# A transformer block with expert retrieval: one dense block's keys and gates brought forward in the last group, six shared PSUM banks

## The chip, the cores and the metric

The kernel runs on one core of a Trainium2 chip. The metric is the device time of one execution in microseconds. The engines are TensorE (PE; its weight loads are PEld), VectorE (DVE), ScalarE (ACT), GpSimd (POOL) and SyncE (SP), which here only issues transfers. Each engine works through its own instructions in order. All times of engines below are from one profiled execution.

## The reference

One block over 1024 tokens of width 1024. The first half mixes tokens (an mLSTM and a differential attention side by side); the second half, which matters here, is a retrieval of experts:

```python
y = jnp.concatenate([hm, od], axis=-1) @ w_out[l]
x = x + g1 * y
h2 = rmsnorm(x, norm2_g[l]) * (1.0 + sc2) + sh2
x = x + g2 * peer(h2, ...)

def block(xb):                      # 128 tokens
    q = (xb @ w_query).reshape(128, 8, 2, 128)
    s = jnp.einsum('thpk,hpnk->thpn', q, sub_keys)
    sv, si = lax.top_k(s, 16)
    cand = sums of all 16 x 16 pairs;  fv, fpos = lax.top_k(cand, 16)
    eidx = jnp.take_along_axis(cidx, fpos, axis=-1)
    g = jax.nn.softmax(fv, axis=-1)
    u = u_tab[eidx]
    act = gelu(jnp.einsum('td,thkd->thk', xb, u))
    return jnp.einsum('thk,thkd->td', g * act, v_tab[eidx])
```

Each token has 8 heads, each head picks 16 of 16384 experts (128 x 128 product keys), and each expert is one row of u and one of v. The result goes through a last rmsnorm.

## The kernel before

The 1024 tokens are 8 blocks tb of 128, worked in three groups of 2, 3 and 3 blocks (GROUPS). A group runs through the front: norm1 (its `dr` at line 357), projections (`ps_pj`, lines 391 and 411, weights `wr` loaded by SyncE), convolution and mLSTM, attention in units that each end with an operation `ae` (line 606) and its transposes `ps_at` (line 617), output projection, norm2 (again `dr`), and product keys: queries, scores `ps_s` (line 862), the tops of 16 per half (lines 891 to 895) and `route`, which yields each token's expert numbers and gates.

Experts are computed in two ways. The blocks tb 0, 1, 6 and 7 gather: GpSimd fetches rows of u and v (`gu`, `gv`, `gvr`), VectorE takes the products with u (line 1010), and the sums with v are done on TensorE (`ga`, line 1072) for tb 0 and 1 and on VectorE for 6 and 7 (line 1046). The blocks tb 2 to 5 (DENSE) are computed against all 16384 experts in the dense phase, which starts when the front has ended. For each of 128 rows j of 128 experts: `s_mm` loads u, splits it into two parts `us` (lines 1312 and 1313), runs 24 matmuls `ps_dS` (line 1320) and a Gelu; `s_gate` multiplies the result by the gates `Gt` and splits it into `W`; `v_step` loads and splits v (`dvs`) and runs the matmuls `ps_dA` (line 1352). Products run 14 rows ahead (AHEAD) of the gates.

The dense phase wants gates as a full matrix, tokens by experts, with zeros for what was not picked. `gates()` makes it from the picked numbers: for each block, after a transposition `ps_gt`, 32 steps of a one-hot `oh` on VectorE (two operations, lines 1237 and 1238, in two buffers), 8 small matmuls `ps_g` (line 1224) and an evacuation into the staging tile `stg` (line 1226), which has one buffer. After every four steps SyncE sends the staging tile, 1 MB, to `G_d` in memory (line 1229). In the front, `gates()` is a background: a generator that is advanced by so many steps at each tick, a tick being a load of weights in a projection. The number per tick is RP. `all_gates` takes the first three dense blocks, tb 2 to 4, in the front; the fourth, tb 5, is in the last group, and its gates are made inside the dense phase, between the first rows of `s_mm`. While that is so, the second part of `us` is made by GpSimd for the first 18 rows, and `Gt` is loaded in two parts.

The front's matmuls write into five PSUM banks (`psb`); a sixth bank (`psq`) belongs to the gates. The order of the instructions on each engine is set when the kernel is built, by a scheduler of the framework that plays the program through on a model of the engines, within the order of priority in which it is written.

Of the kernel before, what the change touches and what calls it, by code (L numbers as in the profile page):

```python
# [8 lines left out]
F32 = mybir.dt.float32  # L9
# [12 lines left out]
P = 128  # L22
# [29 lines left out]
def kernel(ctx: ExitStack, tc: tile.TileContext, x, c_col, ada_w, ada_b, ada_bc, n1c,  # L52
# [3 lines left out]
    WB, T2, C8, KV, T4, RB, SB, OB, WLO, PB, LAG, DB, GD, AHEAD, LG, RH, ORDL, UP, LP, L0, DU, HP, HJ = 7, 8, 4, 2, 3, 3, 1, 2, 0, 5, 4, 2, 1, 14, 3, 4, 1, 18, 310000, 3, 28, 0, 0  # L56
# [13 lines left out]
    RG, RP = 1.6, 1.5  # L70
# [9 lines left out]
    psq = front_ctx.enter_context(tc.tile_pool(name="psq", bufs=6 - PB, space=PSUM))  # L80
# [30 lines left out]
    def gbank(name):  # L111
        return psq.tile([P, 512], F32, tag="pg", name=name)
# [729 lines left out]
    def front_keys(o, found):  # L842

        n, nb = o.n, o.nb
        o.rt = [route_start() for _ in range(nb)]
        for g in range(4):
            if g == N1G and o.k + 1 < len(gs):
                front_norm1(gs[o.k + 1])
# [9 lines left out]
            proj_T(wq, g * 512, o.h2T, nb, q_evac)  # L858
            for b in o.order:
                ps = bank("ps_s")  # L860
                for f in range(4):
                    nc.tensor.matmul(ps[:, f * P:(f + 1) * P], q[f][:, b * P:(b + 1) * P], sk[:, f],
                                     start=True, stop=True)
                if b == o.put_off:
                    if g == 0:
                        kept = fr.tile([P, 16, P], F32, tag="stg", name="s", bufs=SB)
                    s = kept[:, g * 4:g * 4 + 4]
                else:
                    s = fr.tile([P, 4, P], F32, tag="t2", name="s", bufs=T2)
                nc.scalar.activation(s, ps.rearrange("p (f n) -> p f n", f=4), AF.Copy)  # L870
                if b != o.put_off:
                    key_tops(o, b, g, s, found)
        if o.put_off is not None:
            for g in range(4):
                key_tops(o, o.put_off, g, kept[:, g * 4:g * 4 + 4], found)
# [252 lines left out]
    def all_gates():  # L1128
        while gating or not ended:
            if gating and gating[0][2] < sum(tb < starts[-1] for tb in DENSE):  # L1130
                yield from gates(*gating.pop(0))
            elif ended:
                return
# [300 lines left out]
    for k, o in enumerate(gs):  # L1434
# [7 lines left out]
        def found(b, h0=0, nh=PH):  # L1442
            tb, r = o.t0 + b, o.rt[b]
            dense_ = tb in DENSE
            route(r, dense_, tb in MIXED or (dense_ and last), h0, nh)
# [14 lines left out]
        o.put_off = o.order[-1] if k == 0 and DEF else None  # L1460
# [81 lines left out]
```

## Time and profile before

| | us |
|---|---|
| median of 3 runs | 3025.44 (3018.88 to 3027.79) |
| the profiled execution | 3014.83 |
| its span in the trace | 3012.7 |

| engine | busy, us | share of the span |
|---|---|---|
| TensorE | 2795.3 | 93% |
| VectorE | 2382.6 | 79% |
| GpSimd | 1280.1 | 42% |
| ScalarE | 971.3 | 32% |

The profiled execution is one run, and 10.6 us shorter than the median of the others. The span is what the trace covers. A busy share is a mean over stages: the table of stretches further down cuts the last group's front and the dense phase apart. A float32 matmul of the front leaves two records in the trace, and so does a gu; a ps_g, a dS and a dA leave one.

### The profile page before, as it was taken

What the parts mean: (1) busy time and instruction counts of PE and PEld (TensorE: products, weight loads), DVE (VectorE), ACT (ScalarE), POOL (GpSimd) and SP (SyncE); (2) the same over time, 40 slices, a digit from 0 to 9 for tenths busy, and PEclk for the clock granted to TensorE, in tenths of its full rate; (3) what the DMA queues carried; (4) which work ended last, traced back from release to release, by engine and by line L of the source; (5) the groups of instructions that cost most, each with busy time, mean ns of one, the idle gap of its engine ahead of it and who ended that gap; (6) DMA issues with size and microseconds to landing.
All of it is one profiled execution on the core that took longest, in us unless ns stands there. A gap on an engine that the chain in (4) does not pass through costs nothing.

```text
span 3012.7 us, 40060 instructions
## 1 busy us (share of the span) xinstructions
PE 2795.3 (93%) x13686; PEld 2087.7 (69%) x13686; DVE 2382.6 (79%) x5489; ACT 971.3 (32%) x1692; POOL 1280.1 (42%) x1083
## 2 busy tenths in 40 slices
PE   6899999599999989999797999999999999999998
PEld 5547757375566756665475877788777787777886
DVE  5634999847997677356998988899888899888956
ACT  1432244311244444222443322323222223222332
POOL 0000366654565443334556555455444454444300
PEclk9989999699999979999798999999999999999999
DMA  8745699899999887988799999999999999999942
GB/s 281 248 141 178 227 359 331 312 365 337 321 347 323 298 296 275 342 318 312 281 312 321 332 323 320 336 343 322 330 321 335 326 344 321 322 317 311 307 140 70
DMA packets 396848, 900.00 MB, mean 299 GB/s; under 512 B 34770, under 2 KB 184274, under 8 KB 392548
## 3 DMA queue, kind: packets, MB, share of 16 engines
q0 software_dynamic: 147456, 536.94, 49.6%
q1 hardware_dynamic: 249188, 360.51, 35.8%
q8 instruction: 108, 1.77, 0.2%
q14 instruction: 96, 0.79, 0.1%
HBM read 846.97 MB, written 50.35 MB: 298 GB/s over the span
## 4 chain that ended last, share of the span: by engine, by line
PE 44%; DVE 27%; DMA 15%; issue 9%; ACT 2%; POOL 2%; SPq 0%; DVEq 0%; POOLq 0%; ACTq 0%
PE ps_pj L391 10%; PE ps_pj L411 8%; PE ps_dA L1352 7%; DVE gu L1010 7%; DMA Gt<-G_d 6%; PE ps_dS L1320 6%; DVE ga L1046 4%; PE ps_g L1224 3%; PE ga L1072 3%; DMA gu<-in_peer_u_dram,ei 2%; DVE dvs L1346 2%; PE ps_S L593 2%; DVE dacc L1359 2%; DVE us L1313 2%; DVE W L1331 1%
## 5 line engine op out<-in xcount | busy, mean ns | idle before, releaser
L1006 POOL DMA_INDIRECT gu<-in_peer_u_dram,ei x512 | 651.7, 1273 | 958.7 <-DVE sv L894 346.6
L1352 PE MATMUL ps_dA<-dvs,W 128*128 128x512 f32 x2976 | 718.5, 396 | 46.2 <-DVE dvs L1346 18.5
L1320 PE MATMUL ps_dS<-dhT,us 128*128 128x512 f32 x3072 | 733.4, 393 | 11.1 <-POOL us L1313 8.9
L1010 DVE SCALAR_TENSOR_TENSOR gu<-gu,h2r 128x1024 f32<-128x1024 f32 x512 | 630.0, 1241 | 74.6 <-DMA gu<-in_peer_u_dram,ei 66.0
L1352 PEld LDWEIGHTS ps_dA<-dvs,W 128*128 128x128 f32 x2976 | 566.2, 191 | 176.5 <-DVE dvs L1346 22.3
L1320 PEld LDWEIGHTS ps_dS<-dhT,us 128*128 128x128 f32 x3072 | 581.7, 190 | 138.2 <-POOL us L1313 10.3
L1039 POOL DMA_INDIRECT gvr<-in_peer_v_dram,ei x256 | 302.4, 1181 | 314.2 <-DVE ga L1046 178.3
L1058 POOL DMA_INDIRECT gv<-in_peer_v_dram,eT x256 | 274.6, 1073 | 263.1 <-PE ga L1072 143.1
L1046 DVE SCALAR_TENSOR_TENSOR ga<-gvr,w,ga 128x1024 f32<-128x1024 f32 x254 | 325.3, 1281 | 1.5 <-DVE us L1313 0.4
L1345 ACT ACTIVATE dvs<-dv 128x512 fp32r<-128x512 f32 x248 | 155.2, 626 | 323.3 <-PE ps_dA L1352 169.7
L391 PE MATMUL ps_pj<-hT,wr 128*128 128x384 f32 (+1 forms) x768 | 234.7, 461 | 2.8 <-ACT ae L586 2.6
L391 PE MATMUL ps_pj<-h2T,wr 128*128 128x384 f32 (+1 forms) x768 | 231.2, 454 | 0.0
L1321 ACT ACTIVATE ge<-ps_dS 128x512 f32<-128x512 f32 x128 | 76.5, 598 | 441.7 <-PE ps_dS L1320 430.2
L1226 ACT ACTIVATE stg<-ps_g 128x512 f32<-128x512 f32 x128 | 133.9, 1065 | 242.4 <-PE ps_g L1224 162.9
L391 PEld LDWEIGHTS ps_pj<-hT,wr 128*128 128x128 f32 x768 | 145.4, 194 | 79.9 <-issue 9.0
L1329 DVE SCALAR_TENSOR_TENSOR ge<-ge,Gt 128x512 f32<-128x512 f32 x128 | 86.5, 685 | 137.2 <-DMA Gt<-G_d 115.2
L391 PEld LDWEIGHTS ps_pj<-h2T,wr 128*128 128x128 f32 x768 | 142.2, 190 | 74.4 <-issue 11.1
L411 PE MATMUL ps_pj<-wr,hT 128*128 128x256 f32 (+1 forms) x672 | 179.9, 421 | 4.6 <-DMA wr<-in_w_in_dram 3.7
L1346 DVE TENSOR_TENSOR dvs<-dv,dvs 128x512 fp32r<-128x512 f32 x248 | 168.1, 682 | 16.9 <-ACT dvs L1345 16.9
L1237 DVE TENSOR_TENSOR oh<-iotah,dT 128x1024 f16<-128x1024 f16 x128 | 92.0, 724 | 111.7 <-PE ps_g L1224 90.4
L1224 PE MATMUL ps_g<-oh 128*128 128x128 f16 x1024 | 138.6, 296 | 33.3 <-DVE oh L1238 14.5
L1072 PE MATMUL ga<-gv,strip 128*32 128x256 f32 x2048 | 150.7, 410 | 15.4 <-DMA gv<-in_peer_v_dram,eT 11.7
(292 smaller groups left out, 3304.0 us busy)
## 6 DMA issues: line engine op xcount, KB each, us to landing
u<-in_peer_uT_dram SPq DMA_DIRECT2D x128, 512.0 KB
dv<-in_peer_v_dram SPq DMA_DIRECT2D x248, 256.0 KB
wr<-in_w_in_dram SPq DMA_DIRECT2D x168, 256.0 KB
G_d<-stg SPq DMA_DIRECT2D x32, 1024.0 KB
Gt<-G_d SPq DMA_DIRECT2D x15, 2048.0 KB
wmod<-in_ada_w_dram SPq DMA_DIRECT2D x48, 512.0 KB
wr<-in_peer_w_query_dram SPq DMA_DIRECT2D x96, 256.0 KB
wr<-in_w_out_dram SPq DMA_DIRECT2D x48, 256.0 KB
```

Of the source, the lines that this page charges most:

```text
L391: nc.tensor.matmul(out[f], w2[:, kh, f * P:(f + 1) * P], hT[:, kb, :n], start=kb == 0 and f % k == 0, stop=kb == NC - 1 and f % k == k - 1)
L411: nc.tensor.matmul(out[f], hT[:, kb, f * P:(f + 1) * P], wk[:, kh], start=kb == 0 and f % k == 0, stop=kb == NC - 1 and (f % k == k - 1 or ...
L1006: nc.gpsimd.indirect_dma_start(out=u, out_offset=None, in_=pu, in_offset=bass.IndirectOffsetOnAxis(ap=o.ei[:, k:k + 1], axis=0))
L1010: nc.vector.scalar_tensor_tensor(u, u, 1.0, o.h2, op0=OP.mult, op1=OP.mult, accum_out=o.z[:, k:k + 1])
L1039: nc.gpsimd.indirect_dma_start(out=vt, out_offset=None, in_=pv, in_offset=bass.IndirectOffsetOnAxis(ap=o.ei[:, k:k + 1], axis=0))
L1046: nc.vector.scalar_tensor_tensor(o.acc, vt, o.w[:, k:k + 1], o.acc, op0=OP.mult, op1=OP.add)
L1058: got = nc.gpsimd.indirect_dma_start(out=vt, out_offset=None, in_=pv, in_offset=bass.IndirectOffsetOnAxis(ap=o.eT[:, t:t + 1], axis=0))
L1072: mm = nc.tensor.matmul(o.acc[c * 32:(c + 1) * 32, q * QW:(q + 1) * QW], st[:, q, 31 + 32 * i - r:63 + 32 * i - r], vt[:, c * QW:(c + 1) * ...
L1224: nc.tensor.matmul(pg[:, r * P:(r + 1) * P], oh[:, 0, :, r], oh[:, 2 + i, :, r], start=i == 0, stop=i == np_ - 1)
L1320: nc.tensor.matmul(ps, us[:, a, c], hT[:, b, c, sl], start=c == 0 and i == 0, stop=c == NC - 1 and i == 2)
L1346: nc.vector.tensor_sub(vs[:, 1], v, vs[:, 0])
L1352: nc.tensor.matmul(pacc[tb], w[:, a, tb * P:(tb + 1) * P], vs[:, b], start=jj == 0 and i == 0, stop=jj == J - 1 and i == 2)
```

## The change

The front's six banks are one pool, which the gates use too (`gbank = bank`), and RP goes from 1.5 to 2.0. `all_gates` takes every block that is ready, so the gates of tb 5 are made in the front as well, as a background of what remains of the last group's keys. For that, `front_keys` of the last group first calls `keys_alone` for tb 5: the queries of one block as 128 x 512 products with tokens as rows (`proj_R`, evacuated to `qr`), four transposes per head group (`ps_qt`, `qT`), scores and tops, for all four head groups. Then the other two blocks' keys follow as before with 256 tokens in place of 384. The weights of the queries are so loaded twice in the last group, 32 more loads of 256 KB. In the dense phase there are then no gates left to make; by the code that is there, `Gt` is loaded whole and the second part of `us` is made by VectorE for all rows.

```diff
--- before.py
+++ after.py
@@ -53,7 +53,7 @@
                              w_in, conv_w, conv_b, gate_b, mngc, lq1, lk1, lq2, lk2, dngc, w_out,
                              n2c, n2r, wq, skT, pu, puT, pv, fg, out, dbg=None):
     nc = tc.nc
-    WB, T2, C8, KV, T4, RB, SB, OB, WLO, PB, LAG, DB, GD, AHEAD, LG, RH, ORDL, UP, LP, L0, DU, HP, HJ = 7, 8, 4, 2, 3, 3, 1, 2, 0, 5, 4, 2, 1, 14, 3, 4, 1, 18, 310000, 3, 28, 0, 0
+    WB, T2, C8, KV, T4, RB, SB, OB, WLO, PB, LAG, DB, GD, AHEAD, LG, RH, ORDL, UP, LP, L0, DU, HP, HJ = 7, 8, 4, 2, 3, 3, 1, 2, 0, 6, 4, 2, 1, 14, 3, 4, 1, 18, 310000, 3, 28, 0, 0
     MODR = [("oh", OB)] * 4
     XG = 1
     SILU = 2
@@ -67,7 +67,7 @@
     RA = [0.4, 0.4, 0.4]
     RR = [1.0, 1.0, 1.0]
 
-    RG, RP = 1.6, 1.5
+    RG, RP = 1.6, 2.0
     ET = mybir.EngineType
     PACE = ()
     pool = lambda name, bufs, **k: ctx.enter_context(tc.tile_pool(name=name, bufs=bufs, **k))
@@ -77,7 +77,6 @@
     drm = pool("drm", 1, space=DRAM)
     front_ctx = ctx.enter_context(ExitStack())
     psb = front_ctx.enter_context(tc.tile_pool(name="psb", bufs=PB, space=PSUM))
-    psq = front_ctx.enter_context(tc.tile_pool(name="psq", bufs=6 - PB, space=PSUM))
     fg_, fl, fe, fm, ft = (front_ctx.enter_context(tc.tile_pool(name=n, bufs=1)) for n in ("fg", "fl", "fe", "fm", "ft"))
 
     class Front:
@@ -108,8 +107,7 @@
 
     overlapped = []
 
-    def gbank(name):
-        return psq.tile([P, 512], F32, tag="pg", name=name)
+    gbank = bank
 
 
 
@@ -841,10 +839,15 @@
 
     def front_keys(o, found):
 
-        n, nb = o.n, o.nb
-        o.rt = [route_start() for _ in range(nb)]
+        o.rt = [route_start() for _ in range(o.nb)]
+        last = o.k + 1 == len(gs)
+        first = [b for b in o.order if last and o.t0 + b in DENSE]
+        for b in first:
+            keys_alone(o, b, found)
+        rest = sorted(b for b in o.order if b not in first)
+        at, n = rest[0] * P, len(rest) * P
         for g in range(4):
-            if g == N1G and o.k + 1 < len(gs):
+            if g == N1G and not last:
                 front_norm1(gs[o.k + 1])
             sk = o.sk[g // 2][:, g % 2 * 4:g % 2 * 4 + 4]
             q = {}
@@ -855,24 +858,34 @@
                     q[f.start + i] = t[:, i * n:i * n + n]
                 nc.scalar.activation(t[:, :(f.stop - f.start) * n].rearrange("p (f n) -> p f n", n=n), ps, AF.Copy)
 
-            proj_T(wq, g * 512, o.h2T, nb, q_evac)
+            proj_T(wq, g * 512, o.h2T[:, :, at:at + n], len(rest), q_evac)
             for b in o.order:
-                ps = bank("ps_s")
+                if b in rest:
+                    key_scores(o, b, g, [q[f][:, b * P - at:b * P - at + P] for f in range(4)], sk, found)
+
+    def keys_alone(o, b, found):
+
+        for g in range(4):
+            def q_evac(f, ps, c):
+                t = fr.tile([P, 512], F32, tag="t2", name="qr", bufs=T2)
+                nc.scalar.activation(t, ps, AF.Copy)
+                pt = bank("ps_qt")
                 for f in range(4):
-                    nc.tensor.matmul(ps[:, f * P:(f + 1) * P], q[f][:, b * P:(b + 1) * P], sk[:, f],
-                                     start=True, stop=True)
-                if b == o.put_off:
-                    if g == 0:
-                        kept = fr.tile([P, 16, P], F32, tag="stg", name="s", bufs=SB)
-                    s = kept[:, g * 4:g * 4 + 4]
-                else:
-                    s = fr.tile([P, 4, P], F32, tag="t2", name="s", bufs=T2)
-                nc.scalar.activation(s, ps.rearrange("p (f n) -> p f n", f=4), AF.Copy)
-                if b != o.put_off:
-                    key_tops(o, b, g, s, found)
-        if o.put_off is not None:
-            for g in range(4):
-                key_tops(o, o.put_off, g, kept[:, g * 4:g * 4 + 4], found)
+                    nc.tensor.transpose(pt[:, f * P:(f + 1) * P], t[:, f * P:(f + 1) * P], ident)
+                qT = fr.tile([P, 512], F32, tag="t2", name="qT", bufs=T2)
+                nc.scalar.activation(qT, pt, AF.Copy)
+                key_scores(o, b, g, [qT[:, f * P:(f + 1) * P] for f in range(4)],
+                           o.sk[g // 2][:, g % 2 * 4:g % 2 * 4 + 4], found)
+
+            proj_R(wq, g * 512, o.h2T[:, :, b * P:(b + 1) * P], 1, q_evac)
+
+    def key_scores(o, b, g, q, sk, found):
+        ps = bank("ps_s")
+        for f in range(4):
+            nc.tensor.matmul(ps[:, f * P:(f + 1) * P], q[f], sk[:, f], start=True, stop=True)
+        s = fr.tile([P, 4, P], F32, tag="t2", name="s", bufs=T2)
+        nc.scalar.activation(s, ps.rearrange("p (f n) -> p f n", f=4), AF.Copy)
+        key_tops(o, b, g, s, found)
 
     def key_tops(o, b, g, s, found):
 
@@ -1127,7 +1140,7 @@
 
     def all_gates():
         while gating or not ended:
-            if gating and gating[0][2] < sum(tb < starts[-1] for tb in DENSE):
+            if gating:
                 yield from gates(*gating.pop(0))
             elif ended:
                 return
@@ -1442,7 +1455,7 @@
         def found(b, h0=0, nh=PH):
             tb, r = o.t0 + b, o.rt[b]
             dense_ = tb in DENSE
-            route(r, dense_, tb in MIXED or (dense_ and last), h0, nh)
+            route(r, dense_, tb in MIXED, h0, nh)
             if not dense_:
                 if h0 == 0:
                     waiting.append(g_start(tb, r))
@@ -1457,7 +1470,6 @@
         o.order = sorted(range(o.nb), key=lambda b: ((o.t0 + b in DENSE) != (last and ORDL), b))
         o.soon = o.order if SOG[k] else []
         o.part = SOG[k]
-        o.put_off = o.order[-1] if k == 0 and DEF else None
         front_keys(o, found)
         if not last:
             front_T(gs[k + 1])
```

On VectorE, in the last group, the third attention unit's `ae` (L606 before, L604 after) and what stands around it. `oh` is a one-hot of the gates, `gu` a product with gathered rows of u, `ast` and `ae` belong to the attention, `hm`, `num` and `dn` to the mLSTM. Before:

```order
L606 SCALAR_TENSOR_TENSOR ae<-ae,ast 128x896
L1237 TENSOR_TENSOR oh<-iotah,dT 128x1024
L1010 SCALAR_TENSOR_TENSOR gu,z<-gu,h2r 128x1024
L1238 TENSOR_TENSOR oh<-oh,dT 128x1024
L535 TENSOR_TENSOR hm<-num,dn 128x512
L537 SCALAR_TENSOR_TENSOR num,ams<-hm 128x128 x4
L530 TENSOR_SCALAR dn<-num 128x4
L531 TENSOR_TENSOR dn<-dn,num 128x4
```

After, ahead of that `ae`:

```order
L1250 TENSOR_TENSOR oh<-iotah,dT 128x1024
L1251 TENSOR_TENSOR oh<-oh,dT 128x1024
L595 TENSOR_REDUCE ast<-ps_S 128x1
L1023 SCALAR_TENSOR_TENSOR gu,z<-gu,h2r 128x1024
L580 TENSOR_TENSOR ast<-ast 128x1
L581 TENSOR_SCALAR ast<-ast 128x1
L1023 SCALAR_TENSOR_TENSOR gu,z<-gu,h2r 128x1024
L1041 CAST ef_9273<-ei 128x128
```

Before, one pair of `oh` stands between operations of the group's own work; after, pairs of `oh` and `gu` fill the space ahead of the third unit. Counted between the group's norm1 and that unit, 31 `oh` and 48 `gu` became 192 and 96.

On TensorE, where the last group's keys begin. `ps_pj` are the queries, `ps_qt` the new transposes, `ps_s` the scores, `ga` the sums with gathered rows of v. Before:

```order
L1224 LDWEIGHTS oh
L1224 MATMUL ps_g<-oh 128x128
L1072 MATMUL ga<-gv,strip_183 32x256 x16
L391 MATMUL ps_pj<-h2T,wr 128x384 x3
L1224 LDWEIGHTS oh
L1224 MATMUL ps_g<-oh 128x128
```

After:

```order
L1085 MATMUL ga<-gv,strip_180 32x256 x8
L409 MATMUL ps_pj<-wr,h2T 128x512 x7
L1085 MATMUL ga<-gv,strip_180 32x256 x16
L409 MATMUL ps_pj<-wr,h2T 128x512
L1085 MATMUL ga<-gv,strip_179 32x256 x8
L874 MATMUL ps_qt<-ident,qr 128x128 x4
L885 MATMUL ps_s<-sk,qT 128x128 x4
```

Before, the queries of all three blocks run in one sweep beside the gates of the earlier dense blocks; after, the queries of tb 5 alone come in runs of eight 512-wide products, each followed by its transposes and scores, and the gates of earlier blocks are done by then.

On TensorE, where the dense phase begins. Before:

```order
L1216 MATMUL ps_gt<-ident,ii 128x128
L1072 MATMUL ga<-gv,strip_183 32x256 x8
L1320 MATMUL ps_dS<-dhT,us 128x512 x23
L1216 MATMUL ps_gt<-ident,ii 128x128
L1320 MATMUL ps_dS<-dhT,us 128x512 x2
L1072 MATMUL ga<-gv,strip_183 32x256 x16
L1320 MATMUL ps_dS<-dhT,us 128x512 x9
L1072 MATMUL ga<-gv,strip_182 32x256 x8
L1320 MATMUL ps_dS<-dhT,us 128x512 x15
L1072 MATMUL ga<-gv,strip_182 32x256 x8
L1320 MATMUL ps_dS<-dhT,us 128x512 x19
```

After:

```order
L389 MATMUL ps_pj<-h2T,wr 128x256 x24
L885 MATMUL ps_s<-sk,qp 128x128 x4
L389 MATMUL ps_pj<-h2T,wr 128x256 x9
L885 MATMUL ps_s<-sk,qp 128x128 x4
L389 MATMUL ps_pj<-h2T,wr 128x256 x23
L885 MATMUL ps_s<-sk,qp 128x128 x8
L1333 MATMUL ps_dS<-dhT,us 128x512 x384
L1365 MATMUL ps_dA<-dvs,W 128x512 x16
L1333 MATMUL ps_dS<-dhT,us 128x512 x10
```

Before, the transposes `ps_gt` and then the gates of tb 5 stand among the first dS; after, the last `ps_g` stands two rows above the first of these, and 384 dS follow one another up to the first dA.

## Rows read from the trace of the kernel before

**Rows 1.** The page: busy time, share of the span, instructions, of TensorE

```profile
PE 2795.3 (93%) x13686; PEld 2087.7 (69%) x13686; DVE 2382.6 (79%) x5489; ACT 971.3 (32%) x1692; POOL 1280.1 (42%) x1083
```

**Rows 2.** Stretches: us, busy (xrecords) of PE, PEld, DVE, ACT, POOL; clock, DMA share, GB/s

```profile
741.00:955.00 214.00, 207.86 (x1108) 126.07 (x1107) 194.22 (x756) 75.99 (x119) 112.35 (x97) 0.99 0.94 331
955.00:1260.40 305.40, 282.95 (x1901) 201.90 (x1899) 201.71 (x489) 126.58 (x267) 136.24 (x121) 0.92 0.86 304
1260.40:1417.00 156.60, 155.54 (x1064) 95.81 (x1064) 92.56 (x467) 42.09 (x57) 61.22 (x61) 1.00 0.88 312
1417.00:1466.00 49.00, 28.71 (x250) 16.00 (x242) 41.54 (x205) 21.74 (x22) 24.66 (x23) 0.65 0.91 328
1466.00:1700.00 234.00, 196.60 (x1045) 155.27 (x1045) 213.20 (x359) 90.54 (x107) 141.72 (x93) 0.91 0.89 305
1700.00:2900.00 1200.00, 1172.00 (x5084) 962.02 (x5082) 1056.44 (x1419) 359.94 (x540) 556.72 (x453) 0.99 0.91 319
```

**Rows 3.** Timeline: start us, us, what [idle before <-what ended it]

```profile
740.26 0.28 DVE L357 TENSOR_SCALAR dr<-ident,r 128x128 f32<-128x128 f32 x1
...
954.82 1.28 DVE L606 SCALAR_TENSOR_TENSOR ae<-ae,ast 128x1024 f32<-128x1024 f32 x1
...
1260.39 0.67 DVE L357 TENSOR_SCALAR dr<-ident,r 128x128 f32<-128x128 f32 x3
...
1465.30 0.79 PE L1320 MATMUL ps_dS<-dhT,us 128*128 128x512 f32 x1 [0.19 <-ACT us L1312]
...
1638.78 1.22 PE L1352 MATMUL ps_dA<-dvs,W 128*128 128x512 f32 x2 [12.55 <-ACT W L1330]
```

**Rows 4.** Stretches, VectorE on line 1237 (oh) alone: us, busy (xrecords), clock, DMA

```profile
741.00:955.00 214.00, 10.85 (x16) 0.99 0.94 331
955.00:1260.40 305.40, 34.96 (x51) 0.92 0.86 304
1260.40:1466.00 205.60, 19.94 (x29) 0.92 0.89 316
```

**Rows 5.** The same, VectorE on line 1010 (gu) alone

```profile
741.00:955.00 214.00, 58.62 (x96) 0.99 0.94 331
955.00:1260.40 305.40, 56.37 (x92) 0.92 0.86 304
```

**Rows 6.** Timeline, evacuations (ACT, line 1226) and staging transfers (SyncE, line 1229)

```profile
857.96 1.06 ACT L1226 ACTIVATE stg<-ps_g 128x512 f32<-128x512 f32 x1 [1.31 <-PE ps_g L1224]
...
965.10 0.34 SPq L1229 DMA_DIRECT2D G_d<-stg  x1
...
972.35 1.03 ACT L1226 ACTIVATE stg<-ps_g 128x512 f32<-128x512 f32 x1 [1.02 <-DMA G_d<-stg]
...
1282.50 0.34 SPq L1229 DMA_DIRECT2D G_d<-stg  x1
...
1292.28 1.03 ACT L1226 ACTIVATE stg<-ps_g 128x512 f32<-128x512 f32 x1 [7.53 <-DMA G_d<-stg]
```

**Rows 7.** Stretches, TensorE on line 1224 (ps_g) alone

```profile
955.00:1260.40 305.40, 56.38 (x408) 0.92 0.86 304
```

**Rows 8.** Stretches, TensorE on line 1072 (ga) alone

```profile
955.00:1260.40 305.40, 45.77 (x608) 0.92 0.86 304
1260.40:1466.00 205.60, 50.91 (x660) 0.92 0.89 316
```

**Rows 9.** Groups by form on TensorE: busy, mean ns | idle before; first row 1250:1500

```profile
L391 PE MATMUL ps_pj<-h2T,wr 128*128 128x384 f32 x256 | 88.7, 493 | 0.0
...
L411 PE MATMUL ps_pj<-wr,hT 128*128 128x512 f32 x96 | 46.5, 630 | 3.7 <-DMA wr<-in_w_in_dram 3.7
```

**Rows 10.** Stretches, TensorE on line 1320 (dS), then on line 1352 (dA)

```profile
1466.00:1700.00 234.00, 122.96 (x484) 0.91 0.89 305
...
1466.00:1700.00 234.00, 36.24 (x140) 0.91 0.89 305
```

**Rows 11.** A stretch of group 1's attention, columns as in rows 2

```profile
560.00:580.00 20.00, 10.76 (x31) 6.83 (x31) 17.58 (x38) 4.07 (x12) 15.00 (x13) 0.50 0.86 301
```

## Prediction

> **What bounds the kernel now.** I read the page first: TensorE is busy for 93% of the span [rows 1], so the time is nearly TensorE's work plus the little it idles. Where it idles is then read from the table of stretches [rows 2], cut at the marks in [rows 3]: the last group's norm1 at 740, its third attention unit at 955, its norm2 at 1260.4, the first product of the dense phase (dS) at 1465.3, the first dA at 1638.8. The reader is to see there: 741 to 955 loses 6 us on TensorE, 955 to 1260 loses 22, the keys lose almost nothing up to 1417 and 20 us from 1417 to 1466, where the clock granted is 0.65; 1466 to 1700 loses 37, of which 12.6 are one wait for the first gated weights W [rows 3]; the steady dense phase loses 28 in 1200. Together about 125 us since 741. VectorE is the second engine: 194.2 of 214 us in the first stretch, 213.2 of 234 at the entry into the dense phase, but only 201.7 of 305 and 92.6 of 157 between [rows 2]. So the change can win at 1417 to 1700, and must pay with VectorE's time somewhere else.
>
> **The change, part by part.** The sum is made against the profiled execution, 3014.83 us, which lies 10.6 us under the median of 3025.44 that the result will be set against.
>
> *Where the gates of the first three dense blocks go.* On VectorE, between the last group's norm1 and its third attention unit, the order has 161 more one-hot operations (192 in place of 31) and 48 more gu (96 in place of 48), and 5 more of the convolution. All 96 gate steps now stand before that unit; before, they were spread to the end of the keys. VectorE is in order, so all of it is paid there. One oh takes 10.85/16 = 0.68 us [rows 4]; a gu is two records, 58.62/48 = 1.22 us [rows 5]. So 161 x 0.68 = 109, 48 x 1.22 = 59, about 3 for the convolution; on top of the 194.2 that are there already [rows 2] that is 365 us: with VectorE never idle the stretch ends at 741 + 365 = **1106** and not at 955.
>
> Two other queues run beside it. Each group of four gate steps fills the one staging buffer, four evacuations of 1.06 us, and SyncE sends it as 1 MB to memory; the next evacuation waits for the landing. That landing took 7.2 us in one place (965.10 to 972.35) and 9.8 in another [rows 6]. 24 such groups from the first evacuation at 858, at 4 x 1.06 + 7.2 = 11.5 us, end at 858 + 276 = **1134**; at 14.0 us they end at 1195. An evacuation that waits holds ps_g, that holds the one-hot buffers (two), and so the in-order VectorE with the gu queued behind, and the third unit's ae, for which the transposes wait. SyncE's queue has 21 more such issues, each behind its own evacuation, with the projections' weights behind them. And the transfers: 214 us at 331 GB/s are 70.8 MB [rows 2]; 48 gu and some 40 of the gathered v rows, which alternate with gu on GpSimd's queue, of 0.52 MB each (128 x 1024 x 4 bytes), and 21 stagings of 1.05 MB make 139 MB, at the same rate 420 us: **1161**. I take 1130, near the chain of the staging, since the rate of [rows 2] was asked for and not shown to be a ceiling: **+175**, with 1106 and 1161 as ends.
>
> The rate has a rule against it. At 0.94 of the DMA engines' time [rows 2] shows 331 GB/s. The Trainium skill, "Perfetto Trace Analysis", section "Roofline", gives about 435 GB/s as the practical ceiling of a single active core; by that the 139 MB are an estimated 320 us and would end at 1061, so transfers would not bind and VectorE's 1106 would. I keep the bound by the row as the upper end, since at 0.94 the engines have little time left.
>
> *Third unit to norm2.* What remains is 283.0 us of TensorE [rows 2] less the gates that were there (56.4 [rows 7]) and the ga matmuls (45.8 for 608 records, [rows 8]); the order leaves 248 ga matmuls for it, 496 records, 37 us. That is 218, and VectorE has some 201.7 - 2 x 35 - 56.4 = 75 us to do (the oh and gu of [rows 4, 5] taken off [rows 2]), so TensorE binds. Before, 22 us were idle there; most of it waited for gates and gu, which are gone. I take 225 in place of 305.4: **-80**. norm2 then comes at about 1355, 95 later than before.
>
> *The keys.* The dense block's keys alone: 32 matmuls of 128x512, 64 records at 46.5/96 = 31 us; the other two blocks: 256 records with two thirds of the columns of those that took 88.7, 59; together 90 in place of 88.7 [rows 9]. So the added work is hardly matmuls but 16 transposes, 16 evacuations and 32 weight loads of 256 KB (8 MB, 27 us of the stretch's 312 GB/s, in a stretch of 0.88 share): covered by the ga matmuls and by SyncE's lead of several buffers; uncovered, the 27 us show as waits of the projection. What decides is a path: 31 for those keys; VectorE's tops and routing for one block, (92.6 + 41.5 - 2 x 19.9)/3 = 31 [rows 2, 4]; 8 groups of gate steps at 11.5 = 92; and after the last ps_g the order still has 57 of the 128 projection matmuls, 25 us, and scores, 4. That is 183, and TensorE's own work is as much (184.2 [rows 2], ga down from 660 to 560 records, -8 [rows 8]; transposes a few). Above, I bound it by before's 205 plus these 29 at the end: 234. In the middle lies 209, **+4**.
>
> *Dense phase.* The fourth block's gates have left it: 256 records of ps_g, 64 oh, the ga left over, the wait of 12.6 for W, and the 37 idle us of 1466 to 1700. By 1700 dS and dA had done 484 + 140 = 624 records [rows 10] of 6144; at the pace of 1700 to 2900, 5084 in 1200 us, these take 147 and not 234. So 1312.7 + 147 = 1460 in place of 1546.7 is the floor. Against it: before the first W there are 14 to 16 rows of j with only dS, 24 x 0.236 = 5.65 us each, 90 us, and VectorE has in that time, by the order, 42 gu (51), 16 us (18), the last blocks' tops and routes (about 33): 102. The 18 us operations that GpSimd did are VectorE's now, about 1.1 us each, inside that. G loads whole, behind 18 loads of u on SyncE's queue. I give 15 us for it: 1475, **-72**; ends 1461 and 1495.
>
> Six banks for all and the pace of 2.0 change nothing else that I can price; the order holds what they do.
>
> Sum: 175 - 80 + 4 - 72 = **+27**: 3042 on the profiled execution's scale, **3052** against the median.
>
> **The rivals.**
> *A, faster.* VectorE keeps the first stretch saturated: it ends at 1106 (+151); the next takes 218 (-87), the keys 190 (-15), the dense phase 1463 (-84): -35, so 2991. For it: VectorE stood at 0.91 in that stretch with much less queued [rows 2]. Against: the staging chain's 276 us must then start sooner than 858. With the other terms as I took them, the time falls below before's if the first stretch ends before 1103.
> *B, the staging buffer.* If the landings take 9.8 us in a stretch where DMA share is 0.94, the chain ends at 1195 and not at 1130: +65, and 3117. For it: the row of 9.8 stood at a share of 0.88 [rows 2, 6]; against: 7.2 stood inside the crowded stretch.
> *C, the clock.* Without the gates TensorE has less between the attention units. In 560 to 580, the group before, with no gates, it is busy for 10.8 of 20 us at a clock of 0.50, with VectorE at 17.6 [rows 11]. If 80 of the 225 us ran so, that would add 40: 3092. Against it: VectorE was full with gu there, and now it has only 75 us of work. The Trainium skill, "TensorE: Matmul & The Clock Gate", section "HAM oscillation — how this bites in real kernels", says that idle gaps drop the clock to half and that the work after them starts slow; the 0.50 in [rows 11] agrees, and the rule would favour this rival if gaps came.
> *D, nothing to measure.* Gains and losses cancel: 3025. Each term's error is about as large as the sum, so this is not far-fetched.
> That the change does not do what it says is excluded by the order.
>
> **How the numbers follow.** 0.3% or 9 us is about what a measurement of this kernel can tell from no change. Forecast (3035 to 3075) 0.41; A (below 3016) 0.25; D 0.17; C 0.10; B 0.07. Slower is 0.41 + 0.10 + 0.07 = 0.58, same 0.17, faster 0.25. The likeliest, slower case has its own range of 3035 to 3120. The range for 8 in 10 takes in most of A and all of C: 2988 to 3108; left out are B and the lower end of A.
>
> **What would show it.** Right: in the changed kernel's trace the third unit's ae at 1106 to 1161 with VectorE above 0.9 from 741 on; norm2's dr about 225 later; the first dS about 205 to 215 after that; no ps_g after the first dS, and no wait of 12 us before the first dA. Wrong: the third unit before 1100, which says that VectorE or the transfers ran faster than here; evacuations waiting for G_d by more than 60 us in all, which is B; a clock near 0.5 between the third unit and norm2, which is C; dS starting much more than 234 after norm2, which says that the fourth block's gates are the path.

## The result and the profile after

The changed kernel takes 3119.70 us (median of 4 runs, 3107.86 to 3122.86) against 3026.61 (median of 4 runs of the kernel before, 3018.88 to 3036.35): a ratio of 1.030, 95% interval 1.026 to 1.034. The direction was right, the size was not: 93 us instead of 27, above the range of 2988 to 3108 and at the very end of the slower case's own range, 3035 to 3120. The profiled execution took 3122.86 us.

First the page, the line of [rows 1]:

```profile
PE 2815.3 (90%) x13766; PEld 2109.1 (68%) x13766; DVE 2377.9 (76%) x5507; ACT 972.9 (31%) x1694; POOL 1229.8 (39%) x1065
```

TensorE does 20 us more work in a span that is 108 us longer. The marks of [rows 3] in the changed kernel (timeline: start, duration, engine, line, operation):

```profile
735.18 0.27 DVE L355 TENSOR_SCALAR dr<-ident,r 128x128 f32<-128x128 f32 x1
...
1172.98 1.28 DVE L604 SCALAR_TENSOR_TENSOR ae<-ae,ast 128x1024 f32<-128x1024 f32 x1
...
1394.89 0.28 DVE L355 TENSOR_SCALAR dr<-ident,r 128x128 f32<-128x128 f32 x1
...
1632.83 0.80 PE L1333 MATMUL ps_dS<-dhT,us 128*128 128x512 f32 x1 [18.20 <-ACT us L1325]
...
1750.65 1.22 PE L1365 MATMUL ps_dA<-dvs,W 128*128 128x512 f32 x2 [20.53 <-ACT W L1343]
```

And the stretches between them, with the columns of [rows 2]:

```profile
735.00:1173.00 438.00, 352.88 (x2156) 222.06 (x2155) 355.90 (x1034) 157.54 (x204) 217.35 (x193) 0.80 0.91 325
1173.00:1395.00 222.00, 211.15 (x1374) 150.24 (x1372) 86.13 (x281) 77.13 (x215) 61.89 (x62) 0.97 0.66 221
1395.00:1551.00 156.00, 131.03 (x961) 80.21 (x962) 89.47 (x361) 38.34 (x49) 65.61 (x67) 0.89 0.95 352
1551.00:1632.80 81.80, 57.51 (x343) 49.35 (x341) 60.18 (x335) 27.15 (x33) 0.00 (x0) 0.82 0.49 164
```

Norm1 to the third unit takes 438 us for 214.6, the third unit to norm2 222 for 305.6, norm2 to the first dS 238 for 204.9, the rest 1488.3 for 1547.4. In the first of these VectorE was to be the limit; it did 355.9 us of work there, close to the 365 of the sum, but in 438 us, a share of 0.81. TensorE is idle for 85 us of it, at a mean clock of 0.80. So neither engine is full, and the question was what both waited for.

The 85 us are not spread evenly. TensorE's timeline of the changed kernel around 800 us, where the gates begin:

```profile
791.66 6.72 PE L389 MATMUL ps_pj<-hT,wr 128*128 128x384 f32 x20
798.31 1.07 PE L1085 MATMUL ga<-gv,strip 128*32 128x256 f32 x16
802.68 1.07 PE L1085 MATMUL ga<-gv,strip 128*32 128x256 f32 x16 [3.30 <-DMA gv<-in_peer_v_dram,eT]
...
824.30 0.48 PE L1229 MATMUL ps_gt<-ident,ii 128*128 128x128 f32 x1
...
842.89 1.94 PE L1085 MATMUL ga<-gv,strip 128*32 128x256 f32 x16 [4.61 <-DMA gv<-in_peer_v_dram,eT]
847.64 0.47 PE L1229 MATMUL ps_gt<-ident,ii 128*128 128x128 f32 x1 [2.81 <-DVE ii L967]
...
853.26 2.06 PE L1237 MATMUL ps_g<-oh 128*128 128x128 f16 x16 [2.70 <-DVE oh L1251]
...
873.45 2.75 PE L389 MATMUL ps_pj<-hT,wr 128*128 128x384 f32 x4
```

From 798 to 873 there is not one projection matmul. Between the transposes `ps_gt` TensorE has only `ga`, most of which wait for their gathered rows, until VectorE's route delivers `ii` at 847.6 and with it the last `ps_gt` and, at 853.3, the first `ps_g`. In the kernel before, 780 to 860 held 76 us of TensorE work, 57 of them projections. The stretch of 780 to 860 in the kernel before, then in the changed kernel, then its second half (columns as in [rows 2]):

```profile
780.00:860.00 80.00, 76.08 (x417) 48.74 (x418) 75.83 (x343) 24.30 (x33) 43.49 (x39) 0.98 0.95 338
...
780.00:860.00 80.00, 39.35 (x274) 21.80 (x275) 75.03 (x321) 20.59 (x22) 55.46 (x46) 0.63 0.90 317
820.00:860.00 40.00, 15.04 (x118) 6.61 (x119) 37.16 (x117) 8.83 (x8) 30.34 (x26) 0.50 0.92 325
```

The order of TensorE's work shows what is missing there. Projections (`ps_pj`) between the first `ps_gt` and the first `ps_g`, in the kernel before, then in the changed kernel (us, busy, records, clock, DMA):

```profile
827.00:856.80 29.80, 24.19 (x91) 1.00 1.00 366
...
824.30:853.20 28.90, 0.00 (x0) 0.50 0.94 340
```

The way from the first `ps_gt` to the first `ps_g` takes 29 to 30 us in both. Before, 91 records of projections stand in it; after, none.

The granted clock follows: 0.63 here in the mean of these 80 us, and 0.50, the lower of its two levels (1.2 GHz), from 820 to 860, where TensorE is busy for 15 of 40 us. The Trainium skill, "TensorE: Matmul & The Clock Gate", section "HAM oscillation — how this bites in real kernels", says that waits between bursts of matmuls throttle the clock, so that the next burst starts slow; the trace agrees: a `ga` of 16 records takes 1.07 us at 798 and 1.93 us from 808 on, between the waits.

### The profile page after: what moved, and what is told of

Same layout as the page of the kernel before. It is cut to its first block, busy times and chain, and to the rows that moved or that the text cites. A ratio compares the mean times of both kernels' runs of the same rounds, so it can differ in the third digit from the quotient of the medians.

```text
span 3121.1 us, 40321 instructions
## 1 busy us (share of the span) xinstructions
PE 2815.3 (90%) x13766; PEld 2109.1 (68%) x13766; DVE 2377.9 (76%) x5507; ACT 972.9 (31%) x1694; POOL 1229.8 (39%) x1065
## 4 chain that ended last, share of the span: by engine, by line
PE 39%; DVE 23%; DMA 19%; issue 13%; POOL 4%; ACT 2%; SPq 0%; DVEq 0%; POOLq 0%; ACTq 0%
PE ps_pj L389 9%; PE ps_pj L409 8%; DMA Gt<-G_d 7%; PE ps_dA L1365 6%; DVE gu L1023 6%; PE ps_dS L1333 4%; DVE ga L1059 4%; DMA gv<-in_peer_v_dram,eT 3%; DMA gu<-in_peer_u_dram,ei 3%; PE ga L1085 2%; PE ps_g L1237 2%; DMA gvr<-in_peer_v_dram,ei 2%; DVE dvs L1359 2%; POOL gvr L1052 2%; DMA wmod<-in_ada_w_dram 2%
## 5 line engine op out<-in xcount | busy, mean ns | idle before, releaser
L1019 POOL DMA_INDIRECT gu<-in_peer_u_dram,ei x512 | 659.8, 1289 | 983.4 <-DVE sv L907 333.1
L1365 PE MATMUL ps_dA<-dvs,W 128*128 128x512 f32 x2976 | 715.1, 395 | 54.5 <-ACT W L1343 20.5
L1333 PE MATMUL ps_dS<-dhT,us 128*128 128x512 f32 x3072 | 725.7, 391 | 23.2 <-ACT us L1325 19.2
L1023 DVE SCALAR_TENSOR_TENSOR gu<-gu,h2r 128x1024 f32<-128x1024 f32 x512 | 618.1, 1220 | 73.1 <-DMA gu<-in_peer_u_dram,ei 53.8
L1071 POOL DMA_INDIRECT gv<-in_peer_v_dram,eT x256 | 263.4, 1029 | 383.3 <-PE ga L1085 194.7
L1085 PE MATMUL ga<-gv,strip 128*32 128x256 f32 x2048 | 162.4, 437 | 63.7 <-DMA gv<-in_peer_v_dram,eT 58.3
L389 PE MATMUL ps_pj<-h2T,wr 128*128 128x256 f32 (+1 forms) x768 | 202.4, 420 | 0.0
L389 PEld LDWEIGHTS ps_pj<-h2T,wr 128*128 128x128 f32 x768 | 144.8, 192 | 47.6 <-issue 4.1
L1237 PEld LDWEIGHTS <-oh 128*128 128x128 f16 x1024 | 111.2, 120 | 88.0 <-DVE oh L1251 61.4
L1239 ACT ACTIVATE stg<-ps_g 128x512 f32<-128x512 f32 x128 | 123.8, 1083 | 148.8 <-DMA G_d<-stg 89.8
```

Of the source, the lines that this page charges most:

```text
L389: nc.tensor.matmul(out[f], w2[:, kh, f * P:(f + 1) * P], hT[:, kb, :n], start=kb == 0 and f % k == 0, stop=kb == NC - 1 and f % k == k - 1)
L1019: nc.gpsimd.indirect_dma_start(out=u, out_offset=None, in_=pu, in_offset=bass.IndirectOffsetOnAxis(ap=o.ei[:, k:k + 1], axis=0))
L1023: nc.vector.scalar_tensor_tensor(u, u, 1.0, o.h2, op0=OP.mult, op1=OP.mult, accum_out=o.z[:, k:k + 1])
L1071: got = nc.gpsimd.indirect_dma_start(out=vt, out_offset=None, in_=pv, in_offset=bass.IndirectOffsetOnAxis(ap=o.eT[:, t:t + 1], axis=0))
L1085: mm = nc.tensor.matmul(o.acc[c * 32:(c + 1) * 32, q * QW:(q + 1) * QW], st[:, q, 31 + 32 * i - r:63 + 32 * i - r], vt[:, c * QW:(c + 1) * ...
L1237: nc.tensor.matmul(pg[:, r * P:(r + 1) * P], oh[:, 0, :, r], oh[:, 2 + i, :, r], start=i == 0, stop=i == np_ - 1)
```

## Experiments

Two theories stood at the start beside the one in the prediction. T1: the shared pool. Banks of one pool come round in the order in which the program asks for them, so once projections and gates ask the same pool, their orders are tied. T2: the pace of 2.0, or the keys alone with the fourth block's gates in the front. T3 is the prediction's chain: each group of four gate steps waits for the staging buffer's landing.

All stretches below come from each kernel's own profile. Norm1, norm2 and dS are the last group's marks as above; ratios are against the kernel before on the same chip. In the diffs, constants that the kernel sets together in one line are written one by one, and lines around an edit are left out.

| kernel | norm1 | norm1 to norm2 | norm2 to dS | dS to end | ratio (95%) |
|---|---|---|---|---|---|
| before | 740.3 | 520 | 205 | 1547 | |
| changed | 735.2 | 660 | 238 | 1488 | 1.030 (1.026 to 1.034) |
| pool alone | 733.8 | 661 | 157 | 1573 | 1.035 (1.032 to 1.039) |
| changed, one own bank | 739.8 | 519 | 221 | 1543 | 1.003 (1.001 to 1.005) |
| changed, small buffers | 729.7 | 661 | 240 | 1482 | 1.031 (1.026 to 1.035) |
| the same, two staging buffers | 728.7 | 666 | 353 | 1469 | 1.062 (1.057 to 1.067) |
| changed, gates 40 steps later | 734.8 | 629 | 246 | 1490 | 1.022 (1.019 to 1.026) |
| changed, pace 1.0 | 737.6 | 635 | 226 | 1488 | 1.020 (1.017 to 1.024) |
| 20 steps later, pace 1.0 | 739.3 | 590 | 236 | 1488 | 1.009 (1.006 to 1.012) |
| one own bank, keys together | 737.5 | 516 | 206 | 1579 | 1.011 (1.008 to 1.014) |
| one own bank, us on GpSimd | 741.4 | 518 | 221 | 1556 | 1.005 (1.002 to 1.008) |
| two own banks | 764.7 | 567 | 214 | 1480 | 1.001 (0.999 to 1.003) |
| two own banks, lent to the front | 737.1 | 572 | 213 | 1482 | 0.994 (0.991 to 0.996) |
| one own bank, lent to the front | 749.5 | 505 | 213 | 1575 | 1.004 (1.003 to 1.006) |

### The pool alone, and everything but the pool

```diff
-    PB = 5
+    PB = 6
-    psq = front_ctx.enter_context(tc.tile_pool(name="psq", bufs=6 - PB, space=PSUM))
-    def gbank(name):
-        return psq.tile([P, 512], F32, tag="pg", name=name)
+    gbank = bank
```

> The kernel before with one edit: the gates take their banks from the front's pool, now of six, instead of a bank of their own. Theory T1 (the shared pool): banks of one pool come round in the order in which the program asks for them, so projections and gates are tied to each other's order; the gates move ahead of the last group's third attention unit, that stretch grows from 214 us to about 420 to 440, the next shrinks from 305 to about 225, and the time is about 3090 to 3150. Theory T2 (the pace of 2.0, or the keys alone with the fourth block's gates in the front): this kernel has neither, so it stays at about 3027. Theory T3 (the one staging buffer's landings): as T1 in size, but only if the gates move.

The second is the same edit backwards, in the changed kernel:

```diff
-    PB = 6
+    PB = 5
+    psq = front_ctx.enter_context(tc.tile_pool(name="psq", bufs=6 - PB, space=PSUM))
-    gbank = bank
+    def gbank(name):
+        return psq.tile([P, 512], F32, tag="pg", name=name)
```

> The changed kernel with one part undone: five banks for the front and one bank of their own for the gates, as before; keys alone, the fourth block's gates in the front and the pace of 2.0 stay. T1: norm1 to third unit back at about 214 us, third unit to norm2 at about 305, the keys longer than 238 by up to 60 because 61 gate steps instead of 32 are left for them, the dense phase at about 1480 to 1490; in all 3020 to 3060. T2: the first stretch stays near 430 and the time near 3120.

The pool alone makes the whole loss: 3128.02 us, and 661 us from norm1 to norm2, as in the changed kernel. Everything else without the pool gives 3034.68, and 519. T2 falls. TensorE's hole stands in the first and not in the second, in the same 80 us (columns as in [rows 2]):

```profile
780.00:860.00 80.00, 39.71 (x284) 21.87 (x282) 75.69 (x317) 21.62 (x24) 54.59 (x46) 0.63 0.90 314
```

is the pool alone, and

```profile
780.00:860.00 80.00, 75.86 (x417) 48.17 (x418) 74.64 (x333) 23.91 (x33) 41.93 (x38) 0.98 0.96 342
```

is the changed kernel with an own bank. VectorE does the same work in both. There are six banks in both, five and one or six shared, so it is the sharing. The pace of 2.0 changes nothing with an own bank: 31 one-hots stand between norm1 and the third unit at 1.5 and at 2.0. With the shared pool it matters: 154 at 1.5 (pool alone), 192 at 2.0.

Two sizes were not as expected. With the pool alone the first stretch was 406 us and the next 255, not 420 to 440 and 225. With the own bank the keys took 221 us, where 238 to 298 were expected, and the dense phase 1543, not 1480 to 1490.

### Two staging buffers

The second buffer needs room, so both runs have six weight buffers (WB) and six scratch buffers (T2) for seven and eight, and differ in the staging buffers (the list of the first places in memory then counts two for `stg`):

```diff
-    SB = 1
+    SB = 2
```

> The changed kernel with six weight buffers for seven and six scratch buffers for eight, the reference for the run with two staging buffers: it should be near the changed kernel, 3110 to 3150, first stretch 430 to 460.

> The same with two staging buffers, paid for by those small buffers. T3 (each group of four gate steps waits for the landing of the one before): 24 groups at about 10 us in place of 13.6, so the stretch from norm1 to the third unit falls by 60 to 90 us against the run with small buffers and one staging buffer, and the evacuations' waits for the transfer, 51.7 us, go. T1: the waits go, but the stretch falls by under 25 us, since ps_g, projections and gathered sums still stand in one order on TensorE.

ScalarE's waits from 735 to 1395 show the landing in the changed kernel (us in total, times, longest):

```profile
ACT stg L1239 <- DMA G_d<-stg: 51.7, 11, 9.4
```

In the kernel with small buffers and one staging buffer they are

```profile
ACT stg L1239 <- PE ps_g L1237: 58.9, 22, 9.5
ACT stg L1239 <- DMA G_d<-stg: 47.6, 9, 9.0
```

With two buffers no line of the landing is left among ScalarE's waits, the first is

```profile
ACT stg L1239 <- PE ps_g L1237: 134.8, 54, 10.1
```

and norm1 to norm2 is 666 us for 661. So T3 falls, and with it the rival of the staging buffer, although its forecast of 3117 was within 3 us of the median. The landings are waited for, but what ps_g waits for next costs as much. That this kernel is slower by 96 us than the one with small buffers is another matter, after the last scores:

```profile
1615.62 2.07 PE L885 MATMUL ps_s<-sk,qp 128*128 128x128 f32 x16
1748.07 0.80 PE L1333 MATMUL ps_dS<-dhT,us 128*128 128x512 f32 x1 [130.38 <-ACT us L1325]
```

TensorE stands for 130 us for the dense phase's first u. Why the larger staging buffer holds that load back (other memory under the dense phase's tiles would be one way) was not tried.

### Where the gates stand in the program

```diff
             if gating:
+                if gating[0][2] == 0:
+                    for _ in range(40):
+                        yield True
                 yield from gates(*gating.pop(0))
```

> The changed kernel, shared pool kept, but the first dense block's gates are taken up 40 background steps (20 weight loads) later in the program. T1 in its narrow form: with one pool, a projection that asks for a bank after the gates' transposes can't run before these, and they wait for the block's route on VectorE until about 850 us; so TensorE idles from 780 to 860 (25 + 15 of 80 us busy, clock 0.50). Written 40 steps later, the first transposes come after 78 more projection matmuls (542 for 464 in the order), the hole closes (busy above 65 of 80), norm1 to norm2 falls from 660 us to 610 to 630, and the time to 3070 to 3095. Rival T4: VectorE's work and the staging in that stretch set the pace whatever the order, so the hole moves and norm1 to norm2 stays within 15 us of 660.

And, alone:

```diff
-    RG, RP = 1.6, 2.0
+    RG, RP = 1.6, 1.0
```

> The changed kernel with a pace of 1.0 in place of 2.0. The order shows the first gates at the same place (464 projection matmuls ahead), but 104 one-hots in place of 192 ahead of the third unit. T1 narrow: the hole from 780 to 860 stays, busy about 40 of 80; norm1 to norm2 is 640 to 665, about 3105 to 3125. T4 or T2 (too many gates packed ahead of the third unit): the first stretch falls with the gates, norm1 to norm2 to below 620, time below 3090.

The first closes the hole, and norm1 to norm2 falls by 31 us (3094.39 us in all):

```profile
780.00:860.00 80.00, 74.77 (x392) 47.44 (x392) 74.72 (x317) 23.23 (x30) 42.39 (x39) 0.98 0.95 335
```

The pace of 1.0 leaves the hole as it was,

```profile
780.00:860.00 80.00, 39.47 (x280) 21.78 (x284) 73.83 (x329) 17.87 (x21) 52.95 (x47) 0.63 0.90 313
```

and still takes 25 us from norm1 to norm2 (3085.70 us in all). The stretch of 635 us is below what T1 in its narrow form allowed and above what the other side wanted; the time in all is the other side's, below 3090. So there are two losses: the hole, and one that grows with how densely the gates are packed among projections and attention. The hole goes with the order as read above: between the first `ps_gt` and the first `ps_g` the pool alone and the pace of 1.0 have no projections, as the changed kernel, while the own bank has 91 records of them and the later gates 37. Both edits together, with a wait of 20 steps:

> Shared pool, with both of the edits that helped one by one: the first gates 20 steps later, which at a pace of 1.0 is again 20 weight loads, and the pace of 1.0. Alone, the wait took 31 us from norm1 to norm2 and the pace 23. If they are two separate losses of the shared rotation (the hole before the first gates, and the packing of gates among the projections), they add: norm1 to norm2 600 to 610, about 3055 to 3075 in all. If they are the same loss, it stays at 625 to 640 and 3080 to 3100.

590 us and 3054.41: they add, and a little more (31 + 25 = 56, measured 69). The two edits may not be quite independent, since a later start also moves later gates; that was not tried apart. All 192 one-hots of the first three blocks are ahead of norm2 in all of these, so 69 of the 140 us are the gates' place among the other work alone.

### The keys alone

```diff
-        first = [b for b in o.order if last and o.t0 + b in DENSE]
+        first = []
```

> The kernel with the gates' own bank, and the fourth block's gates still in the front, but its keys together with the other two blocks' as before, not alone. If bringing the keys forward is worth what it is meant for, the fourth block's gates start some 60 us later here and the first dS comes 20 to 60 us later after norm2 than the 221 us of the kernel with keys alone: 3045 to 3085. If not, because the earlier blocks' gates fill that time anyway, it is 3020 to 3040, like it.

3053.86 us for the 3034.68 with keys alone. The first dS came earlier here (206 us after norm2, not 241 to 281: that expectation missed, though the time lay in its range), but the dense phase took 1579 us for 1543: the fourth block's last `ps_g` comes 384 us after norm2 instead of 365, and the first dA 417 instead of 400. Counted from norm2 to the end, keys alone gain 21 us: the part of the change that gave it its name does what it is for. With one own bank and keys alone it is not enough: 61 gate steps are left after norm2, and TensorE waits 34.2 us for the first W.

One edit of the dense phase, with the own bank and keys alone:

```diff
-            (nc.gpsimd if j < UP and gating else nc.vector).tensor_tensor(us[:, 1], u, us[:, 0], op=OP.subtract)
+            (nc.gpsimd if j < UP else nc.vector).tensor_tensor(us[:, 1], u, us[:, 0], op=OP.subtract)
```

> The kernel with the gates' own bank and keys alone, and the second part of us again on GpSimd for the first 18 rows of the dense phase, as in the kernel before. If VectorE is what delays the first W there (gathered products, tops and 18 us operations of 1.14 us), the dense phase gets 10 to 25 us shorter than 1543: 3010 to 3025. If the load of the gates (24 us in the changed kernel) is it, nothing changes: 3030 to 3040.

3036.86, no gain: VectorE's 18 operations are not what delays the first W. The trace points to the matrix of the gates: here the last staging transfer is issued at 1638.5, the load of `Gt` at 1645.4, and the first dA starts at 1670.7 after a wait of 33.3 us.

### Own banks, as many as the gates need

```diff
-    PB = 6
+    PB = 4
+    psq = front_ctx.enter_context(tc.tile_pool(name="psq", bufs=6 - PB, space=PSUM))
-    gbank = bank
+    def gbank(name):
+        return psq.tile([P, 512], F32, tag="pg", name=name)
```

> The changed kernel with two banks of their own for the gates and four for the front, in place of six shared. The order keeps the first ps_gt away from the projections and has all 192 one-hots of the first three blocks ahead of norm2, but only 56 ahead of the third unit. T1 (the shared rotation costs, not the gates' early place as such): norm1 to norm2 is 520 us plus the 34 us of ps_g moved ahead, 545 to 575; the keys, with 32 steps left, 200 to 240; the dense phase 1480 to 1500; in all 2990 to 3040. T4 (so many gates ahead of norm2 cost 140 us whatever the banks): norm1 to norm2 about 640 to 660, in all 3090 or more.

All of the first three blocks' gates are ahead of norm2 here too, and norm1 to norm2 is 567 us, not 660. So gates ahead of norm2 need not cost more than 47 us, of which some 34 are the ps_g that moved (248 at 56.4/408 us, [rows 7]), and the other 93 come with the shared pool. Most of these 93 are again the gates' place: 56 one-hots stand ahead of the third unit here, 192 in the changed kernel. The shared pool with both edits above had 64 there, and 590 us; against that, own banks gain 23. The keys take 214 and the dense phase 1480 us. What is lost is at the start: norm1 comes 24 us later. Until the first gate is made, two of six banks lie idle, so the next kernel lends them:

```diff
+    begun, turn = [], [0]
     def bank(name):
+        turn[0] += 1
+        if not begun and turn[0] % 3 == 0:
+            return gbank(name)
         return psb.tile([P, 512], F32, tag="b", name=name, bufs=PB - PJ)
 def gates(...):
+        begun.append(True)
```

> The kernel with two own banks for the gates and four for the front, but as long as no gates are made (the first two groups' fronts and the second group's keys) every third bank of the front comes from the gates' two. The kernel with four and two reached the last group's norm1 25 us later than the kernel before (764.7 for 740.3), and from there on took 2261 us for 2272. If the four banks made it late, norm1 is back at 735 to 742, the rest stays at about 2261, and the time is 3000 to 3015, faster than both. If something else did (the order of priorities, the pace), norm1 stays at 755 to 765 and the time at about 3028.

3006.42 us (3001.63 to 3016.20): a ratio of 0.994, interval 0.991 to 0.996, so 0.6% faster than the kernel before and well ahead of the changed one. Its stretches from norm1 to norm2, to dS, and to the end:

```profile
737.00:1309.00 572.00, 531.65 (x3253) 364.37 (x3251) 434.08 (x1310) 235.55 (x420) 256.15 (x224) 0.93 0.87 306
1309.00:1522.00 213.00, 188.22 (x1381) 124.05 (x1381) 144.60 (x695) 61.79 (x77) 86.03 (x84) 0.91 0.94 342
1522.00:3003.00 1481.00, 1432.04 (x6338) 1166.44 (x6337) 1279.14 (x1828) 451.58 (x678) 657.43 (x528) 0.99 0.89 310
```

Norm1 is back at 737, norm1 to norm2 is 572 us, so the 567 did not hang on the late norm1, and the dense phase keeps its gain of 66 us on the kernel before. The same with five banks and one:

```diff
-    PB = 4
+    PB = 5
-        if not begun and turn[0] % 3 == 0:
+        if not begun and turn[0] % 6 == 0:
```

> The same with five banks and one, every sixth of the front's from the gates' bank until gates are made. The kernel with one own bank stood at 739.8 at norm1 and 3035 in all; the sixth bank can give back up to 5 us there (the shared pool of six stood at 735), and the fourth block's gates still reach into the dense phase: 3025 to 3035. If the sixth bank's rotation delays the front instead, it is above 3035.

3039.08 us. Norm1 is 10 us later than without the lending (749.5 for 739.8), so here it delays the front, and the fourth block's gates still reach into the dense phase.

## Why the prediction was wrong

**Norm1 to the third unit**, +175 as taken, was +223. The work was sized right (VectorE 356 for 365 us), but 365 us in the 389 that I took is a share of 0.94, and measured it is 0.81. The step that failed is the sentence on six banks for all, that they "change nothing else that I can price; the order holds what they do". The pool alone takes norm1 to norm2 to 661 us, and everything but the pool leaves it at 519. Of the 140 us the sum had 95, since it took the gates' early place from the order; it lacked TensorE's hole, which took 37 us of work out of 780 to 860 (39.4 for 76.1), and whose closing gave back 31. The order did hold it: in the changed kernel no projection stands between the first `ps_gt` and the first `ps_g`, before 91 records. I counted VectorE's rows there, and not what TensorE was left with while `ps_gt` waited for the route.

**The rates** were read as bounds that they are not. 1161 was the upper end, by the DMA rate of [rows 2]; the stretch ended at 1173. Its bytes and its mean rate came out near that term (142 MB at 325 GB/s for 139 at 331), so the time alone does not refute it. But the rate was no ceiling: the kernel before ran at 392 GB/s from 840 to 860, inside that very stretch, and the changed kernel at 388 from 935 to 955 and at 402 from 1420 to 1440. Nor were the transfers fuller in the hole: 317 GB/s at a share of 0.90 there, 338 at 0.95 in the same 80 us before. The Trainium skill, "Perfetto Trace Analysis", section "Roofline", gives about 435 GB/s as the ceiling of a single active core; of all stretches of 20 us, cut at multiples of 20, in the traces here the highest is at 411 (1260 to 1280 with five banks, one lent).

**Third unit to norm2**, -80: measured -84. This term held, and so did its reason, that TensorE binds there (211 of 222 us busy).

**The keys**, +4: measured +33, 4 us above the upper bound. With two own banks the keys take 214 and 213 us, near the 209 of the sum, so about 24 us of the miss come with the shared pool. After the last scores TensorE stands 18.2 us for the first `us`, which my path did not have; with two own banks, lent, it is 1.1:

```profile
1521.75 0.49 PE L1341 MATMUL ps_dS<-dhT,us 128*128 128x512 f32 x1 [1.07 <-ACT us L1333]
```

The two ends are not quite the same, since there the last `ps_g` comes 19 us after the first dS, and in the changed kernel 48 us before it. Why the first `us` comes late was not tried.

**The dense phase**, -72: measured -59, within its bounds. The wait for the first W, which was to go, did not: it is 20.5 us for 12.6. The term had allowed 15 us of friction, and the phase came out 13 above that. SyncE's queue shows the cause that the term named (start, duration, line, transfer):

```profile
1646.40 78.24 SPq L1323 DMA_DIRECT2D u<-in_peer_uT_dram  x14
1724.69 0.43 SPq L1280 DMA_DIRECT2D Gt<-G_d  x1
```

The last staging transfer was issued at 1587, but the load of the gates stands behind 14 loads of u in this stretch.

Added up on the profiled execution: 45 us too little from norm1 to norm2, 29 for the keys, 13 for the dense phase, less 5 by which norm1 came sooner: 82 for the 81 by which the forecast of 3042 missed (3122.86), the rest rounding. Of the rivals, the clock's rival named a place where it did not happen (0.97 between the third unit and norm2); the clock fell before, in the hole. The staging buffer's rival had the time and the wrong cause: the evacuations waited 51.7 us for landings, under its own sign of 60. One row was misread there: the landing of 7.2 us (965 to 972) stands in the stretch of [rows 2] with a DMA share of 0.86, not in the crowded one at 0.94.

**What is shown and what is argued.** That the sharing causes the loss, and that moving the gates in the program removes about half of it, the runs show. That two own banks, with the same gates ahead of norm2 but fewer of them ahead of the third unit, lose 47 and not 140 us, they show too. That the hole stands where no projection is between `ps_gt` and `ps_g`, and nowhere else, is read from the traces. That this order comes from the rotation of banks in the order of the program is argued from the code and fits all of them; no run looked at a bank. Why the shared pool still costs some 20 us with the gates at about the same place stays open.

## What to carry to other kernels

A background task that may wait long for its input should not draw its buffers from the pool of the work that it is to hide under: give it its own, and try how many; two of six were right here. Lending them to the main work until it starts gave back 28 us at norm1 with two banks and cost 10 with one, so that has to be tried too. When a change alters who shares a pool, compare the order of the engine that is to stay full around the first place where the sharer can stall, and not only the order of the engine that gets more work. A forecast of the right time is no evidence for its mechanism; take the suspected wait away.

## What was not expected of the hardware

The DMA engines moved 402 GB/s from 1420 to 1440 in the changed kernel, where rows of several hundred us show 304 to 331 at shares of 0.86 to 0.94; a share near 0.9 is thus no sign that the rate can't rise. The share itself reads 1.04 there, so it is no fraction that ends at 1. And a wait removed can leave the time as it is: 47.6 us of landings went with the second staging buffer, and norm1 to norm2 was 666 for 661.
